# Two transformer-like blocks on one core: the first block's mixers in another order, row-half products as pairs

## The chip, the cores and the metric

The kernel runs on one core of a Trainium2 chip. The metric is the device time of one execution in microseconds (us); the time before is 1532.46 us, the median of three runs (1527.14 to 1532.51). The profile is of one further execution.

## The reference

`reference()` runs `first_block` and then `second_block` on 256 tokens of width 1024, all in float32. `first_block` has two layers, each like this (cut):

```
proj = h @ w_in[l]
nq, nkv, ngate, gq, gk, gv, glr, gog, pu = split(proj)
mixed = concatenate([nsa_mixer(nq, nkv, ngate, ...),
                     gla_mixer(gq, gk, gv, glr, gog, ...),
                     pool_mixer(pu, ...)])
h  = layer_norm(ALPHA * h + mixed @ w_out[l])
ff = square(relu(h @ w_up[l])) @ w_down[l]
h  = layer_norm(ALPHA * h + ff)
```

- `nsa_mixer` (sparse attention; 6 query heads in 2 groups of 3, head size 64) adds three gated attentions per query: over 15 compressed key blocks (a small two-layer network on 32 tokens each), over selected key blocks, and over a window. With 256 tokens all selected blocks and the whole window are kept, so the second and third are plain causal attention, each with its own keys and values.
- `gla_mixer` (linear attention; 6 heads, key size 32, value size 64, chunks of 64 tokens) computes per chunk masked scores times values, adds the decayed queries times the state carried from the chunks before, normalizes, and multiplies by `silu(og)`.
- `pool_mixer` is a windowed mean and a small product.

`second_block` works on 272 tokens: a layer of gated recurrence with windowed attention (16 heads), a mamba2 layer, and a convolutional feed-forward in each.

## The kernel before

**Dense products.** Every product with a large weight is done in three matmuls on split numbers (`mm3`, L273 to L275: high by high, low by high, high by low). A weight piece is loaded by SyncE's one DMA queue into `raw` (3 buffers), ScalarE rounds it to its high part `wh` (L258) and VectorE subtracts to get the low part `wl` (L259), 6 buffers each. `weights()` fixes the order of the pieces, and each `wchunk` call in the code must take the next one. Each `mm3` on 128x128x256 takes one k-slice of a product; 8 of them make a column group of the input projection.

**The mixers' stage of a layer** computes the input projection in groups: `tok(n)` gives a token-major result (1: query, 0: keys, 2: values of the sparse attention, 3: values `gv` of the linear attention), `fm(n)` a feature-major one (8: gate input, 0: values to be compressed, 4 to 6: the output gate `og`). `hooks` are functions called between the k-steps of a group; `behind` wraps them in `issue_after(self.pe.ins)`, which makes everything issued in them stand after the last dense product in the order. Around the change the code reads:

```
tok(2, ..., {HOOKS[3]: blocks, HOOKS[4]: hidden, HOOKS[6]: lambda: self.gla_ends(gq, G)})
tok(3, ..., {HOOKS[5]: compressed})
self.gla_back(l, G, gv, gos)
self.nsa(l, qT, kT, vsb, vc, sg, mh, ml)
for p in range(3): fm(4 + p, ...)        # then gate, times gos, split into mh, ml
self.gemm(a[f"wouta{l}"], 5, 2, mh[:, 0:5], ...)
self.gemm(a[f"woutb{l}"], 3, 4, mh[:, 5:8], ...)
```

So `gla_back` and `nsa` are written in one piece each, and the scheduler, which orders each engine's instructions by their readiness, fills the gaps with dense products of `fm(4..6)` and of `wouta` as it can. `wouta` needs the pooled and linear parts of `mixed`, `woutb` the sparse attention.

**The thin products**, those that use a part of TensorE's rows or columns. `gla_back`: chunk sums (L874, 64x64), scores (L892, 32 rows: `ge` by `gx`), values and states (L902, L908), sums of squares (L916). `nsa`, for each half t of the queries and each head h: scores of the two groups g=0 and g=1 (L796, 64 rows each, at rows 0 to 63 and 64 to 127, into the PSUM banks `a` and `d`), exponentials on VectorE (L801, L805, L806, L811) and ScalarE (L803), transposes (L755), copies of the transposed (L816), and the outputs (L820, 64 columns per group). The second block's attention does its scores in the same two row halves (L1420).

Of the kernel before, what the change touches and what calls it, by code (L numbers as in the profile page):

```python
# [143 lines left out]
def weights(a):  # L144
# [35 lines left out]
class Kern:  # L180
# [267 lines left out]
    def mix1(self, l, h, xh, xl, finish):  # L448
# [57 lines left out]
        def fm(n, evac):  # L506
            (wh, wl), = self.wchunk(a[f"winf{l}"][n])
            ps = self.mbank()[:, :256]
            for k in range(8):
                s = slice(k * 128, k * 128 + 128)  # L510
                self.mm3(ps, wh[:, s], wl[:, s], xh[:, k], xl[:, k], k == 0, k == 7)
            evac(ps)
# [100 lines left out]
        ksb = p1.tile([128, 2, 6, 64], F32, name="ksb", tag="gos")  # L613
        tok(0, lambda t, ps: A.activation(ksb[:, t].rearrange("p a b -> p (a b)"), ps[:, :384], AF.Copy),
            {HOOKS[0]: front, HOOKS[1]: lambda: to_T(qT, qsb), HOOKS[2]: pooled})
        rope(ksb)
        kT = p1.tile([128, 3, 256], F32, name="kT", tag="kT")
        vcT = p1.tile([128, 256], F32, name="vcT", tag="vcT")
        fm(0, lambda ps: A.activation(vcT, ps, AF.Copy))

# [42 lines left out]

        vsb = p1.tile([128, 2, 256], F32, name="vsb", tag="vsb")
        tok(2, lambda t, ps: A.activation(vsb[:, t], ps[:, :256], AF.Copy), {HOOKS[3]: blocks, HOOKS[4]: hidden, HOOKS[6]: lambda: self.gla_ends(gq, G)})
        gv = p1.tile([128, 2, 384], F32, name="gv", tag="tb")
        tok(3, lambda t, ps: A.activation(gv[:, t], ps[:, :384], AF.Copy), {HOOKS[5]: compressed})
# [4 lines left out]
        big = p1.tile([128, 2048], F32, name="big", tag="cw1")  # L672
        gs = big[:, 0:768].rearrange("p (a t) -> p a t", a=3)
        for p in range(3):
            og = w1.tile([128, 256], F32, name="og", tag="og")
            fm(4 + p, lambda ps, og=og: A.activation(og, ps, AF.Copy))
# [3 lines left out]
            V.tensor_tensor(gs[:, p], gs[:, p], gos[:, p], op=OP.mult)  # L680
            self.split(mh[:, 2 + p], ml[:, 2 + p], gs[:, p])
# [6 lines left out]
        self.gemm(a[f"wouta{l}"], 5, 2, mh[:, 0:5], ml[:, 0:5], first, shift)  # L688
# [3 lines left out]
    def gemm(self, chunks, nk, per, xh, xl, sink, shift=None, N=256, bank=None):  # L692
# [59 lines left out]
    def nsa(self, l, qT, kT, vsb, vc, sg, mh, ml):  # L752
# [5 lines left out]
        for t in range(2):  # L758
            W = 128 * (t + 1)
            q = slice(t * 128, t * 128 + 128)  # L760

            P = w1.tile([128, 6, 16], F32, name="pc", tag="pc")
            sc = self.bank()
            for h in range(3):
                mm(sc[:, h * 32:h * 32 + 32], lhsT=qT[:, h, q], rhs=self.kcb, start=True, stop=True)
# [12 lines left out]
            o = self.bank("c")  # L778
            ct = self.bank()
            tr(ct[0:96, 0:128], P.rearrange("p s n -> p (s n)"))  # L780
# [3 lines left out]
            mm(o[:, 0:384], lhsT=vc, rhs=self.cTb.rearrange("p h q -> p (h q)"), start=True, stop=False,  # L784
               skip_group_check=True)
            nb = 2 * (t + 1)
            for h in range(3):

                sp = [self.bank(x) for x in ("a", "d")]
                P = (w1.tile([128, 512], F32, name="P", tag="P", bufs=3),  # L790
                     p1.tile([128, 512], F32, name="Pg", tag=f"tb{h % 2}"))
                m = w1.tile([128, 2, 2], F32, name="m2", tag="m2", bufs=4)
                sm = w1.tile([128, 2, 2], F32, name="s2", tag="s2", bufs=4)
                for b in range(2):
                    for g in range(2):
                        mm(sp[g][:, b * W:b * W + W], lhsT=qT[gp[g], h, q], rhs=kT[gp[g], 1 + b, 0:W], start=True, stop=True)  # L796
                for b in range(2):
                    for g in range(2):
                        c = slice(b * W, b * W + W)

                        V.tensor_tensor_reduce(P[g][:, c], sp[g][:, c], nm[:, 128 * t:128 * t + W], scale=-0.125,  # L801
                                               scalar=3.0e38, op0=OP.add, op1=OP.min, accum_out=m[:, b, g:g + 1])
                        A.activation(P[g][:, c], P[g][:, c], AF.Exp, scale=-1.0, bias=m[:, b, g:g + 1],  # L803
                                     accum_out=sm[:, b, g:g + 1])
                V.reciprocal(sm, sm)  # L805
                V.tensor_tensor(sm, sm, view(sg, t * 18 + 6 + 2 * h, [[6, 2], [1, 2]]), op=OP.mult)  # L806
                PT = []
                for g in range(2):
                    for b in range(2):
                        c = slice(b * W, b * W + W)  # L810
                        V.tensor_scalar(P[g][:, c], P[g][:, c], sm[:, b, g:g + 1], None, op0=OP.mult)  # L811
                    pt = self.bank("b")
# [3 lines left out]
                    A.activation(PT[g][:, :2 * W], pt[:, :2 * W], AF.Copy)  # L816
                for j in range(nb):
                    b, kb = j // (t + 1), j % (t + 1)
                    for g in range(2):
                        mm(o[gp[g], h * 128:h * 128 + 128], lhsT=vsb[:, kb, b * 128 + g * 64:b * 128 + g * 64 + 64],  # L820
                           rhs=PT[g][:, j * 128:j * 128 + 128], start=False, stop=j == nb - 1, skip_group_check=True)
            ov = o[:, 0:384].rearrange("p (h q) -> p h q", h=3)
            self.split(mh[:, 5:8, q], ml[:, 5:8, q], ov)
# [41 lines left out]
    def gla_back(self, l, G, gv, gos):  # L865
# [4 lines left out]
        for n in range(3):  # L870
            b = self.bank()
            r = slice((n % 2) * 64, (n % 2) * 64 + 64)
            for p in range(3):
                mm(b[0:64, p * 128:p * 128 + 128], lhsT=kt[r, n // 2, p * 64:p * 64 + 64],  # L874
                   rhs=gv[r, n // 2, p * 128:p * 128 + 128], start=True, stop=True)
            for i in range(2):
                d = slice(i * 32, i * 32 + 32)
                o = S[d, n, :, i * 64:i * 64 + 64]
                ds = b[d, 0:384].rearrange("p (a v) -> p a v", a=3)[:, :, i * 64:i * 64 + 64]
# [910 lines left out]
```

## Time and profile before

| what | before |
|---|---|
| median of three runs | 1532.46 us (1527.14 to 1532.51) |
| the profiled execution | 1528.76 us |
| its span in the trace | 1526.8 us (2.0 us lie outside) |
| TensorE busy | 1498.2 us, 98% of the span |
| VectorE, ScalarE busy | 1121.6 us (73%), 989.3 us (65%) |
| mixers' stage, layer 1 | 35.43 to 144.12 us: 108.69 us at a mean granted clock of 0.92 |
| mixers' stage, layer 2 | 365.99 to 478.71 us: 112.72 us at 0.88 |

Busy time of TensorE says that a matmul was under way, not that the array worked at its full rate: the granted clock (1.00 is 2.4 GHz, 0.50 is 1.2 GHz) and the shape of the products decide how much was done in it. The two stages go from the first 384-wide product of `tok(1)` to the first product of `woutb`.

### The profile page before, as it was taken

How to read it: one execution, taken by the hardware profiler on the slowest of the kernel's cores; microseconds unless marked ns; L12 is line 12 of the kernel's file. 1: busy time of each engine (PE TensorE's matmuls, PEld its weight loads, DVE VectorE, ACT ScalarE, POOL GpSimd, SP SyncE). 2: the span in 40 equal slices, each digit the busy share in tenths (PEclk: the TensorE clock that was granted, in tenths of full speed). 3: DMA queues.
4: the chain of work that ended last, by engine and by line, in shares of the span. 5: the costliest groups of instructions: out<-in, count | busy, mean ns of one | idle time of the engine just before them, and what ended most of it. 6: DMA issues, size and time to landing. Idle time of an engine off the chain costs nothing.

```text
span 1526.8 us, 29217 instructions
## 1 busy us (share of the span) xinstructions
PE 1498.2 (98%) x11685; PEld 1420.7 (93%) x11685; DVE 1121.6 (73%) x2237; ACT 989.3 (65%) x1922; POOL 3.2 (0%) x11
## 2 busy tenths in 40 slices
PE   8999999999999999999999999999999999999998
PEld 8878999999879999999977999999989999999998
DVE  5847976559657965568774799854898896899853
ACT  5646854448456754457866598754799795598752
POOL 0000000000000000000000000000000000000000
PEclk9979999999889999999989999999999999999999
DMA  7503465545313555445331345544455544345551
GB/s 257 192 21 132 150 219 184 193 159 170 97 42 137 199 190 190 173 162 198 118 111 56 138 164 195 167 175 146 145 190 210 171 138 158 139 148 194 205 176 52
DMA packets 43559, 239.05 MB, mean 157 GB/s; under 512 B 6272, under 2 KB 11296, under 8 KB 20384
## 3 DMA queue, kind: packets, MB, share of 16 engines
q1 hardware_dynamic: 42912, 235.39, 44.6%
q8 instruction: 91, 1.49, 0.4%
q10 hardware_dynamic: 512, 1.80, 0.4%
q14 instruction: 44, 0.36, 0.1%
HBM read 236.09 MB, written 1.08 MB: 155 GB/s over the span
## 4 chain that ended last, share of the span: by engine, by line
PE 87%; DVE 5%; ACT 5%; DMA 1%; issue 1%; SPq 0%; DVEq 0%; ACTq 0%
PE mm L273 10%; PE mm L274 10%; PE mm L275 10%; PE a L273 6%; PE a L274 6%; PE a L275 6%; PE c L274 3%; PE c L275 3%; PE c L273 3%; PE b L275 3%; PE b L274 3%; PE b L273 3%; DVE wl L259 1%; PE d L273 1%; PE d L275 1%; PE d L274 1%
## 5 line engine op out<-in xcount | busy, mean ns | idle before, releaser
L259 DVE TENSOR_TENSOR wl<-raw,wh 128x1024 fp32r<-128x1024 f32 (+3 forms) x448 | 518.3, 1163 | 224.5 <-ACT wh L258 216.6
L258 ACT ACTIVATE wh<-raw 128x1024 fp32r<-128x1024 f32 (+3 forms) x448 | 449.8, 1009 | 313.9 <-PE mm L274 130.3
L275 PE MATMUL mm<-xh,wl 128*128 128x256 f32 (+2 forms) x584 | 171.6, 294 | 1.4 <-DVE wl L259 1.4
L273 PE MATMUL mm<-xh,wh 128*128 128x256 f32 (+2 forms) x584 | 170.9, 293 | 2.1 <-ACT wh L258 2.1
L274 PE MATMUL mm<-xl,wh 128*128 128x256 f32 (+2 forms) x584 | 170.6, 292 | 0.0
L275 PEld LDWEIGHTS mm<-xh,wl 128*128 128x128 f32 x584 | 113.2, 194 | 5.3 <-issue 2.4
L273 PEld LDWEIGHTS mm<-xh,wh 128*128 128x128 f32 x584 | 113.0, 194 | 5.3 <-ACT wh L258 3.3
L274 PEld LDWEIGHTS mm<-xl,wh 128*128 128x128 f32 x584 | 112.6, 193 | 3.6 <-issue 2.8
L273 PE MATMUL a<-xh,wh 128*128 128x256 f32 (+2 forms) x376 | 106.5, 285 | 1.7 <-ACT xh L1101 1.5
L274 PE MATMUL a<-xl,wh 128*128 128x256 f32 (+2 forms) x376 | 107.2, 286 | 0.0
L275 PE MATMUL a<-xh,wl 128*128 128x256 f32 (+2 forms) x376 | 106.4, 284 | 0.0
L275 PE MATMUL mm<-hh,wl 128*128 128x256 f32 (+1 forms) x292 | 82.7, 283 | 0.0
L274 PE MATMUL mm<-hl,wh 128*128 128x256 f32 (+1 forms) x292 | 82.6, 283 | 0.0
L273 PE MATMUL mm<-hh,wh 128*128 128x256 f32 (+1 forms) x292 | 82.6, 283 | 0.0
L275 PE MATMUL a<-hh,wl 128*128 128x256 f32 (+1 forms) x280 | 79.3, 283 | 0.0
L273 PE MATMUL a<-hh,wh 128*128 128x256 f32 (+1 forms) x280 | 79.1, 282 | 0.0
L274 PE MATMUL a<-hl,wh 128*128 128x256 f32 (+1 forms) x280 | 79.0, 282 | 0.0
L273 PEld LDWEIGHTS a<-xh,wh 128*128 128x128 f32 x376 | 70.7, 189 | 2.9 <-ACT xh L1101 2.6
L274 PEld LDWEIGHTS a<-xl,wh 128*128 128x128 f32 x376 | 70.8, 188 | 0.5 <-DVE xl L1102 0.2
L275 PEld LDWEIGHTS a<-xh,wl 128*128 128x128 f32 x376 | 70.9, 189 | 0.1
L273 PE MATMUL mm<-sz,wh 128*128 128x258 f32 (+1 forms) x208 | 62.0, 298 | 0.4 <-ACT yn L1130 0.3
L275 PE MATMUL mm<-sz,wl 128*128 128x258 f32 (+1 forms) x208 | 59.2, 285 | 0.6 <-DVE wl L259 0.6
(634 smaller groups left out, 4625.9 us busy)
## 6 DMA issues: line engine op xcount, KB each, us to landing
raw<-fupb SPq DMA_DIRECT2D x40, 1024.0 KB, 4.8
raw<-wdn SPq DMA_DIRECT2D x32, 1024.0 KB, 4.8
raw<-wupb SPq DMA_DIRECT2D x28, 1024.0 KB, 4.8
raw<-bin SPq DMA_DIRECT2D x22, 1024.0 KB, 4.9
raw<-fdna SPq DMA_DIRECT2D x16, 1024.0 KB, 4.8
raw<-ain SPq DMA_DIRECT2D x11, 1024.0 KB, 4.8
raw<-win SPq DMA_DIRECT2D x8, 768.0 KB, 4.9
raw<-fdnb SPq DMA_DIRECT2D x8, 768.0 KB, 4.3
```

The costliest lines, as they stand in the source:

```text
L258: nc.scalar.activation(h, raw[:, s:s + piece], AF.Copy)
L259: nc.vector.tensor_tensor(l, raw[:, s:s + piece], h, op=OP.subtract)
L273: mm(out, lhsT=lh, rhs=rh, start=first, stop=False, **kw)
L274: mm(out, lhsT=lh, rhs=rl, start=False, stop=False, **kw)
L275: self.pe = mm(out, lhsT=ll, rhs=rh, start=False, stop=last, **kw)
```

## The change

Three things change in the first block, for both layers, and one in both blocks.

1. The weight groups stand in another order: `tok(3)` comes before `tok(0)`, `fm(4..6)` before `tok(2)`.
2. `gla_back` returns seven functions (states, then scores, outputs and norms of each half) that are called as hooks inside `fm(0)`, `fm(4..6)` and `tok(2)`; `nsa` becomes a generator whose steps (compressed scores, scores of a head, transposes, outputs) are called inside `tok(2)` and, after the k-steps 1 and 4 of each of the 8 outputs, inside `wouta`'s product (`between`). The scores run two heads ahead of the transposes.
3. In the first half the transposes of both groups go to one bank, and one copy takes them.
4. `pair(f)` emits `f(1)` and makes `f(0)` stand after it. It is used for the scores and outputs of `nsa` and for the second block's scores. The banks of the scores are named per head ("dd", "cb", "da", "ad").

```
@@ weights
         yield f"winf{l}", 8, 1024
+        yield from tok(3)
         yield from tok(0)
-        yield f"winf{l}", 0, 1024
+        for n in (0, 4, 5, 6):
+            yield f"winf{l}", n, 1024
         yield from tok(2)
-        yield from tok(3)
-        for n in (4, 5, 6):
-            yield f"winf{l}", n, 1024
...
+    def pair(self, f):
+        with self.tc.issue_after(f(1).ins):
+            f(0)
...
@@ mixers
-        tok(0, ..., {HOOKS[0]: front, HOOKS[1]: lambda: to_T(qT, qsb), HOOKS[2]: pooled})
...
-        tok(2, ..., {HOOKS[3]: blocks, HOOKS[4]: hidden, HOOKS[6]: lambda: self.gla_ends(gq, G)})
-        tok(3, ..., {HOOKS[5]: compressed})
-        self.gla_back(l, G, gv, gos)
-        self.nsa(l, qT, kT, vsb, vc, sg, mh, ml)
...
+        tok(3, ..., {0: front, 5: lambda: to_T(qT, qsb)})
+        tok(0, ..., {2: pooled, 6: lambda: self.gla_ends(gq, G)})
+        rope(ksb)
+        gla = self.gla_back(l, G, gv, gos)
+        run = lambda *n: lambda: [gla[i]() for i in n]
+        fm(0, lambda ps: A.activation(vcT, ps, AF.Copy), {4: run(0)})
...
+        fm(4, lambda ps: gate(0, ps), {0: run(1), 4: blocks})
+        fm(5, lambda ps: gate(1, ps), {0: run(2), 3: hidden, 6: run(4)})
+        fm(6, lambda ps: gate(2, ps), {0: run(3), 2: run(5), 5: compressed})
+        nsa = self.nsa(l, qT, kT, vsb, vc, sg, mh, ml)
+        step = lambda: next(nsa, None)
+        tok(2, ..., {0: last_gla, 2: step, 4: step, 6: step})
...
-        self.gemm(a[f"wouta{l}"], 5, 2, mh[:, 0:5], ml[:, 0:5], first, shift)
+        self.gemm(a[f"wouta{l}"], 5, 2, mh[:, 0:5], ml[:, 0:5], first, shift, between=lambda: behind(step))
+        for _ in nsa:
+            pass
...
@@ gemm
+                        if between and k in (1, 4):
+                            between()
...
@@ nsa: scores of a head
-                sp = [self.bank(x) for x in ("a", "d")]
+            sp = [self.bank(x) for x in ("dd", "cb", "da", "ad", "ad", "ad")[3 * t + h]]
...
-                for b in range(2):
-                    for g in range(2):
-                        mm(sp[g][:, b * W:b * W + W], lhsT=qT[gp[g], h, q], rhs=kT[gp[g], 1 + b, 0:W], ...)
+            for b in range(2):
+                self.pair(lambda g: mm(sp[g][:, b * W:b * W + W], lhsT=qT[gp[g], h, qs[t]],
+                                       rhs=kT[gp[g], 1 + b, 0:W], ...))
...
@@ gla_back
-            be = [self.bank() for _ in range(2)]
+            be = [self.bank("da"[1 - t]) for _ in range(2)]
...
+        return [states, on(scores, 0), on(outputs, 0), on(norms, 0), on(scores, 1), on(outputs, 1), on(norms, 1)]
```

Three places of TensorE's queue, in layer 1, show what moves; a row is line, operation, out<-in, shape, with the engines that it waits for in brackets and the number of equal rows behind. The first is where the linear attention's scores stand. Before (L892: scores of the first half, `d` their bank; L874 chunk sums; L796 sparse-attention scores; L274 and so on dense):

```order
L796 MATMUL a_946<-kT_573,qT_275 128x128
L874 MATMUL d_854<-gv_761,gkt_457 64x128 [waits DVE_49,PE_49,Activation_49]
L874 MATMUL d_854<-gv_761,gkt_457 64x128 x2
L796 MATMUL a_946<-kT_573,qT_275 128x128
L796 MATMUL a_984<-kT_573,qT_275 128x128
L892 MATMUL d_862<-ge_456,gx_454 128x128 [waits DVE_49,PE_49]
L892 MATMUL d_862<-ge_456,gx_454 128x128 x2
L796 MATMUL a_984<-kT_573,qT_275 128x128
L274 MATMUL mm_1233<-xl_75,wh_798 128x256
L275 MATMUL mm_1233<-xh_74,wl_799 128x256
L273 MATMUL mm_1233<-xh_74,wh_798 128x256
L892 MATMUL d_863<-ge_456,gx_454 128x128 [waits DVE_49,PE_49]
```

After, the scores are L967 and the dense products L272 to L274:

```order
L272 MATMUL mm_723<-xh_74,wh_662 128x256
L273 MATMUL mm_723<-xl_75,wh_662 128x256
L274 MATMUL mm_723<-xh_74,wl_663 128x256 [waits DVE_49]
L967 MATMUL a_727<-ge_459,gx_457 128x128 [waits Activation_49]
L967 MATMUL a_728<-ge_459,gx_457 128x128 [waits Activation_49]
L967 MATMUL a_727<-ge_459,gx_457 128x128
L967 MATMUL a_728<-ge_459,gx_457 128x128
L967 MATMUL a_727<-ge_459,gx_457 128x128
L967 MATMUL a_728<-ge_459,gx_457 128x128
L272 MATMUL mm_723<-xh_74,wh_662 128x256
L273 MATMUL mm_723<-xl_75,wh_662 128x256
```

The products of the two banks (727 and 728) alternate, and dense products stand ahead of them and behind them; before, the three of one bank stood together among other thin products.

The second place is the sparse attention's scores of the second half of the queries. Before, the left half of the heads (bank `a`) and, 130 rows later, the right half (bank `d`):

```order
L796 MATMUL a_1085<-kT_573,qT_275 128x256 [waits DVE_49]
L796 MATMUL a_1085<-kT_573,qT_275 128x256
L796 MATMUL a_1131<-kT_573,qT_275 128x256 [waits DVE_49]
L796 MATMUL a_1131<-kT_573,qT_275 128x256
```

```order
L755 MATMUL d_1079<-ident_87,pc_1062 96x128 [waits DVE_49]
L796 MATMUL d_1086<-kT_573,qT_275 128x256 x2
L796 MATMUL d_1132<-kT_573,qT_275 128x256 [waits PE_49,Activation_49]
L784 MATMUL c_1078<-cTb_132,vc_614 128x384 [waits DVE_49]
L796 MATMUL d_1132<-kT_573,qT_275 128x256
L796 MATMUL d_1178<-kT_573,qT_275 128x256 [waits DVE_49]
L796 MATMUL d_1178<-kT_573,qT_275 128x256
```

After (L825 scores, L867 outputs, L777 transposes), one head's scores:

```order
L825 MATMUL d_1237<-kT_429,qT_275 128x256 [waits DVE_49]
L867 MATMUL c_1174<-PT_1221,vsb_436 64x128 [waits Activation_49]
L867 MATMUL c_1174<-PT_1221,vsb_436 64x128 x3
L825 MATMUL a_1236<-kT_429,qT_275 128x256
L825 MATMUL d_1237<-kT_429,qT_275 128x256
L825 MATMUL a_1236<-kT_429,qT_275 128x256
L777 MATMUL b_1260<-ident_87,pc_1112 96x128 [waits DVE_49,PE_49]
```

The two halves of a head, 1236 and 1237, now stand in one place; in this head another head's outputs stand behind the first of the four.

The third place is one head inside `wouta`'s product. Before (L755 transposes, L820 outputs):

```order
L755 MATMUL b<-ident,P 128x128 [waits DVE_49]
L755 MATMUL b<-ident,P 128x128
L755 MATMUL b<-ident,P 128x128 [waits DVE_49]
L755 MATMUL b<-ident,P 128x128
L755 MATMUL b<-ident,Pg 128x128 [waits DVE_49,Activation_49]
L755 MATMUL b<-ident,Pg 128x128
L755 MATMUL b<-ident,Pg 128x128 [waits DVE_49]
L755 MATMUL b<-ident,Pg 128x128
L820 MATMUL c<-PT,vsb 64x128
L273 MATMUL mm<-mh,wh 128x256 [waits Activation_49]
L273 MATMUL mm<-mh,wh 128x256
L820 MATMUL c<-PT,vsb 64x128 [waits Activation_49]
L820 MATMUL c<-PT,vsb 64x128 x6
```

After:

```order
L777 MATMUL b<-ident,P 128x128 [waits PE_49,Activation_49]
L777 MATMUL b<-ident,P 128x128 [waits DVE_49]
L777 MATMUL b<-ident,Pg 128x128 [waits DVE_49] x2
L272 MATMUL mm<-mh,wh 128x256
L273 MATMUL mm<-ml,wh 128x256
L274 MATMUL mm<-mh,wl 128x256
L272 MATMUL mm<-mh,wh 128x256
L273 MATMUL mm<-ml,wh 128x256
L274 MATMUL mm<-mh,wl 128x256
L272 MATMUL mm<-mh,wh 128x256
L273 MATMUL mm<-ml,wh 128x256
L274 MATMUL mm<-mh,wl 128x256
L825 MATMUL d<-kT,qT 128x256
L825 MATMUL a<-kT,qT 128x256
```

Before, the transposes of both groups and the outputs follow each other with two dense products among them; now nine dense products and the first scores of another head stand between the transposes and the outputs.

## Rows read from the trace of the kernel before

**Rows 1.** The page's head.

```profile
span 1526.8 us, 29217 instructions
```

**Rows 2.** Busy time by stretch: us, each engine's busy time, granted clock, DMA share, GB/s.

```profile
35.43:46.56 11.13, 11.13 (x64) 9.68 (x61) 9.84 (x20) 7.46 (x16) 0.00 (x0) 1.00 0.86 306
70.22:76.41 6.19, 5.93 (x44) 4.55 (x43) 5.10 (x16) 1.77 (x6) 0.00 (x0) 1.00 0.57 200
76.41:93.48 17.07, 17.07 (x66) 12.35 (x65) 4.30 (x14) 3.75 (x14) 0.00 (x0) 0.50 0.00 0
97.75:134.50 36.75, 35.39 (x249) 26.73 (x248) 25.45 (x112) 26.59 (x81) 0.00 (x0) 1.00 0.22 73
134.50:144.12 9.62, 9.62 (x82) 9.52 (x81) 7.16 (x11) 3.89 (x6) 0.00 (x0) 1.00 0.40 126
407.51:434.81 27.30, 27.30 (x110) 22.18 (x110) 6.96 (x24) 7.16 (x20) 0.00 (x0) 0.50 0.04 9
35.43:144.12 108.69, 106.19 (x734) 88.06 (x732) 72.77 (x210) 61.34 (x155) 0.00 (x0) 0.92 0.34 113
365.99:478.71 112.72, 110.67 (x734) 92.26 (x732) 72.18 (x208) 61.72 (x156) 0.00 (x0) 0.88 0.28 92
```

**Rows 3.** TensorE's timeline, layer 1, 73.7 to 74.6 us: start, us, line, out<-in, count.

```profile
73.73 0.90 PE L892 MATMUL d<-ge,gx 32*128 32x128 f32 x6
74.57 0.48 PE L796 MATMUL a<-kT,qT 64*128 64x128 f32 x2
```

**Rows 4.** TensorE's timeline, layer 1, 104 to 124 us.

```profile
104.32 1.16 PE L796 MATMUL d<-kT,qT 64*128 64x128 f32 x8
105.40 0.39 PE L275 MATMUL mm<-xh,wl 128*128 128x256 f32 x1
...
114.89 0.28 PE L275 MATMUL mm<-mh,wl 128*128 128x256 f32 x1
...
116.79 1.81 PE L796 MATMUL d<-kT,qT 64*128 64x256 f32 x6
118.53 0.91 PE L784 MATMUL c<-cTb,vc 96*128 96x384 f32 x2
119.37 1.56 PE L796 MATMUL d<-kT,qT 64*128 64x256 f32 x6
120.86 0.39 PE L273 MATMUL mm<-mh,wh 128*128 128x256 f32 x1
121.08 0.28 PE L274 MATMUL mm<-ml,wh 128*128 128x256 f32 x1
121.20 0.28 PE L275 MATMUL mm<-mh,wl 128*128 128x256 f32 x1
...
121.74 0.70 PE L755 MATMUL b<-ident,P 128*128 128x128 f32 x4
...
124.51 1.09 PE L820 MATMUL c<-PT,vsb 128*64 128x128 f32 x14
```

**Rows 5.** TensorE's timeline, second block's attention.

```profile
768.73 0.39 PE L1420 MATMUL a<-akT,aqT 64*128 64x272 f32 x1
768.74 0.39 PE L1420 MATMUL d<-akT,aqT 64*128 64x272 f32 x1
768.96 0.39 PE L1420 MATMUL a<-akT,aqT 64*128 64x272 f32 x1
```

**Rows 6.** ScalarE's timeline, layer 1, one head of the second half.

```profile
119.44 0.49 ACT L803 ACTIVATE Pg<-Pg,m 128x256 f32<-128x256 f32 x1
...
122.47 0.60 ACT L816 ACTIVATE PT<-b 128x512 f32<-128x512 f32 x1 [0.80 <-PE b L755]
```

**Rows 7.** VectorE's timeline, the same stretch.

```profile
118.31 0.42 DVE L801 CUSTOM_DVE_ANT_0 Pg<-d,nmask 128x256 f32<-128x256 f32 x1
...
120.45 0.17 DVE L805 RECIPROCAL s<-s 128x4 f32<-128x4 f32 x1
...
121.33 0.61 DVE L811 TENSOR_SCALAR P<-P,s 128x256 f32<-128x256 f32 x2
```

More of the change, by code (lines that the diff above doesn't have):

```diff
@@ L511, in fm @@
                 self.mm3(ps, wh[:, s], wl[:, s], xh[:, k], xl[:, k], k == 0, k == 7)
+                if k in hooks:
+                    behind(hooks[k])
             evac(ps)
@@ L679, in mix1, with gated, last_gla @@
             V.scalar_tensor_tensor(gs[:, p], og, self.v(f"ng{l}", p), gs[:, p], op0=OP.mult, op1=OP.mult)
-            V.tensor_tensor(gs[:, p], gs[:, p], gos[:, p], op=OP.mult)
-            self.split(mh[:, 2 + p], ml[:, 2 + p], gs[:, p])
+        def gated():
+            for p in range(3):
+                V.tensor_tensor(gs[:, p], gs[:, p], gos[:, p], op=OP.mult)
+                self.split(mh[:, 2 + p], ml[:, 2 + p], gs[:, p])
+        fm(4, lambda ps: gate(0, ps), {0: run(1), 4: blocks})
[3 more added lines that the diff above has]
+        step = lambda: next(nsa, None)
+        def last_gla():
+            gla[6]()
+            gated()
+        tok(2, lambda t, ps: A.activation(vsb[:, t], ps[:, :256], AF.Copy), {0: last_gla, 2: step, 4: step, 6: step})
         first, shift, add, stats, finish = self.layernorm(self.nrm, h, f"ln1_g{l}", f"ln1_b{l}", xh, xl, nd=6)
@@ L757, in nsa, with compressed @@
         gp = [slice(g * 64, g * 64 + 64) for g in range(2)]
-        for t in range(2):
-            W = 128 * (t + 1)
-            q = slice(t * 128, t * 128 + 128)
+        qs = [slice(t * 128, t * 128 + 128) for t in range(2)]
+        state, o = {}, {}
+        def compressed(t):
             P = w1.tile([128, 6, 16], F32, name="pc", tag="pc")
-            sc = self.bank()
+            sc = self.bank("b")
             for h in range(3):
-                mm(sc[:, h * 32:h * 32 + 32], lhsT=qT[:, h, q], rhs=self.kcb, start=True, stop=True)
+                mm(sc[:, h * 32:h * 32 + 32], lhsT=qT[:, h, qs[t]], rhs=self.kcb, start=True, stop=True)
             V.scalar_tensor_tensor(P, sc[:, 0:96].rearrange("p (s n) -> p s n", n=16), 0.125,
@@ L783, in nsa, with begin @@
                 A.activation(self.cTb[r, h], ct[r, 0:128], AF.Copy)
[L784 removed]
+        def begin(t):
+            o[t] = self.bank("c")
+            mm(o[t][:, 0:384], lhsT=vc, rhs=self.cTb.rearrange("p h q -> p (h q)"), start=True, stop=False,
                skip_group_check=True)
[L786 to L812 removed]
@@ new lines, in transposes @@
+        def transposes(t, h):
+            W, nb = 128 * (t + 1), 2 * (t + 1)
+            P, PT = state[t, h], []
+            if t == 0:
+                pt = self.bank("b")
+                for g in range(2):
+                    for j in range(2):
+                        tr(pt[:, g * 256 + j * 128:g * 256 + j * 128 + 128], P[g][:, j * 128:j * 128 + 128])
+                T = p1.tile([128, 512], F32, name="PT", tag=("gq", "gk")[h % 2])
+                A.activation(T, pt, AF.Copy)
+                PT = [T[:, 0:256], T[:, 256:512]]
+            else:
+                for g in range(2):
+                    pt = self.bank("bd"[g])
@@ L815, in nsa, with outputs, end @@
                     PT.append(p1.tile([128, 512], F32, name="PT", tag=("gq", "gk")[g]))
[L816 to L823, printed above, removed]
+                    A.activation(PT[g], pt, AF.Copy)
+            state[t, h] = PT
+        def outputs(t, h):
+            nb, PT = 2 * (t + 1), state[t, h]
+            for j in range(nb):
+                b, kb = j // (t + 1), j % (t + 1)
+                self.pair(lambda g: mm(o[t][gp[g], h * 128:h * 128 + 128],
+                                       lhsT=vsb[:, kb, b * 128 + g * 64:b * 128 + g * 64 + 64],
+                                       rhs=PT[g][:, j * 128:j * 128 + 128], start=False, stop=j == nb - 1,
+                                       skip_group_check=True))
+        def end(t):
+            self.split(mh[:, 5:8, qs[t]], ml[:, 5:8, qs[t]], o[t][:, 0:384].rearrange("p (h q) -> p h q", h=3))
+        compressed(0)
+        scores(0, 0)
+        yield
+        scores(0, 1)
+        yield
+        compressed_T(0)
+        compressed(1)
+        yield
+        heads = [(t, h) for t in range(2) for h in range(3)]
+        for i, (t, h) in enumerate(heads):
+            transposes(t, h)
+            yield
+            if h == 0:
+                begin(t)
+            outputs(t, h)
+            if h == 2:
+                end(t)
+            if i + 2 < 6:
+                scores(*heads[i + 2])
+            if i == 1:
+                compressed_T(1)
+            yield
     def gla_front(self, l, gq, gk, glT, wg2, rst):
@@ L1418, in attend @@
                 for i in range(per):
-                    for kv in range(2):
-                        mm(sc[kv][:, i * W:i * W + W], lhsT=qT[KP[kv], hb * 4 + i0 + i, q0:q0 + 128],
-                           rhs=kT[KP[kv], keys[kv]], start=True, stop=True)
+                    self.pair(lambda kv: mm(sc[kv][:, i * W:i * W + W], lhsT=qT[KP[kv], hb * 4 + i0 + i, q0:q0 + 128],
+                                            rhs=kT[KP[kv], keys[kv]], start=True, stop=True))
                 for i in range(per):
```

96 lines of the change are left out of this document (61 added, 35 removed).

## The prediction

> **What bounds the kernel now.** I read the page's head first: the span is 1526.8 us [rows 1], the execution 1528.76 us, so about 2 us lie outside. TensorE is busy for 98% of the span, so a gain must come from TensorE work that becomes shorter, not from idle time that is filled. The busy time by stretch says where it can: the mixers' stage takes 108.69 us in layer 1 and 112.72 us in layer 2, at mean granted clocks of 0.92 and 0.88 [rows 2]. That mean hides two levels. In 76.41 to 93.48 us the clock is 0.50 (1.2 GHz) for 17.07 us, in layer 2 in 407.51 to 434.81 us for 27.30 us; the stretch after is at 1.00 (2.4 GHz) again. In both, TensorE counts as busy for all of the time, while VectorE is busy for 4.30 and 6.96 us, ScalarE for 3.75 and 7.16 us: nothing waits for them for long. In the 6.19 us ahead of the first fall TensorE was busy for 5.93 us at 1.00, but with thin products (the linear attention's 64x64 and 32-row ones, the left halves of the sparse scores) and few dense ones among them [rows 2].
>
> The second loss is in TensorE's timeline. The sparse scores use 64 of 128 rows. The eight 64x128 rows at 104.32 us go on until 105.40, 0.135 us each; the six 64x256 rows at 116.79 until 118.53 and those at 119.37 until 120.86, 0.29 and 0.25 us each [rows 4]: each half pays for the whole array. In the second block the same form, 64 rows by 272, starts in both banks within 0.01 us (768.73 `a`, 768.74 `d`) and the next at 768.96: 0.23 us for two rows [rows 5].
>
> **The change part by part.**
>
> *Weight groups and linear attention as steps.* Nothing is added to TensorE: the dense products are the same, the thin ones too. They are spread: the 64x64 sums, scores, values and norms go into `fm(0)`, `fm(4..6)` and `tok(2)`, with dense products between them. If the clock stays at 1.00, both stretches run in half of their time: (17.07 + 27.30)/2 = 22.2 us gained [rows 2]. Bounds: 0 (it falls elsewhere) and 22.2. I take all of it, because the place that made it fall, a long series of thin products with hardly a dense one, is gone; the nearest series that is left is as short as the one from 115.0 (behind the dense product at 114.89) to 120.86 us, 5.9 us with transposes, outputs and half-row scores and no dense product [rows 4], and the stretch in which it lies kept 1.00 [rows 2].
>
> *Order of the loads.* `tok(3)` moves ahead of `tok(0)`, so that three groups of 384 columns follow each other, about 6 MB together with their neighbours on SyncE's queue. In 35.43 to 46.56 us, where such groups run now, TensorE is busy for 11.13 of 11.13 us with DMA at 0.86 and 306 GB/s [rows 2]: 6 MB take 19.6 us at that rate, about as long as their products. I take 0; without that cover it would cost some 1.5 us.
>
> *Score pairs.* Per layer there are 24 rows of 128 columns at 0.135 us (3.2 us) and 24 of 256 at 0.27 (6.5 us) [rows 4]. A perfect pair costs one row in place of two. In the new order a few heads are split (another head's outputs or transposes stand among the four products), so that the 12 products of a half (three heads, two branches, two groups) take the time of 7 instead of 6. So 5/12 of 9.7 us, 4.05 per layer, 8.1 in all. Bounds: 0 (the halves run one after the other) and 9.7.
>
> *Linear scores alternate.* The six 32-row products at 73.73 us take 0.84 us until 74.57, 0.14 each [rows 3]; 24 per layer are 3.4 us. Now two row groups in two banks alternate. No row shows a 32-row pair, so the bounds are 0 and half of both layers' 6.8, 3.4 us; I take the middle, 1.7, as the 64-row pair of rows 5 is the nearest row and the first pair of each group may start late.
>
> *Output pairs.* The fourteen rows at 124.51 us take 1.09 us, 0.08 each [rows 4]: less than the 0.135 of a score of the same 128 columns, so the column halves overlap already. 0.
>
> *Mode switches.* A dense product behind a thin group starts its successor 0.22 us later (120.86 to 121.08), where dense ones behind each other take 0.12 (to 121.20) [rows 4]: 0.1 us per switch. In the two queues a layer's stage has 31 changes from thin to dense now and 34 before: 0.3 us per layer, which I leave out.
>
> *New waits.* TensorE takes its queue in order, and each head's chain now lies between its scores and its transposes. For a head of the second half it is: a reduce on VectorE of 0.42 us, then four exponentials of 0.49 (the other reduces lie beside them), a reciprocal of 0.17 and a product of that size, and two pairs of scales at 0.61 [rows 6, 7]; 3.9 us, and behind the transposes 0.60 for each copy [rows 6]. What stands on TensorE between a head's scores and its transposes is another head's transposes, four for each group (2 x 0.7) and outputs (1.1), and about fifteen dense products, one output's worth (1.8 at 0.117, from 82 in 9.62 us) [rows 2, 4]: 4.3 us. So cover and chain are nearly equal. ScalarE and VectorE also make the next `wh` and `wl` there. Queued behind a waiting transpose are the dense products of the same output, and behind them everything. Bounds: 0 and 15 us per layer (six heads by 2.5 us, a chain whose half is not covered). I take 2 per layer, 4 in all, as the rows put cover and chain within 0.4 us of each other, a third of a microsecond for each of six heads.
>
> *Copies and second block.* One copy instead of two for three heads per layer saves some 0.5 us of ScalarE off the path: 0. In the second block the halves already start together [rows 5]: 0, plus or minus 1.
>
> Sum: 22.2 + 8.1 + 1.7 - 4 = 28.0 us. Against the profiled execution: 1528.76 - 28 = 1500.8, say **1501 us**. The median shown, 1532.46, is 3.7 us above that execution, so 1501 may be measured up to that much higher; the range holds it. From below it fits: the layer-1 stage would be 108.69 - 8.5 - 4.05 - 0.85 + 2, about 97 us, the layer-2 stage 112.72 - 13.65 - 2.9, about 96: two stages of the same work become equal.
>
> **The rivals.**
> 1. *The clock falls at another place* (a series of linear steps behind each other, or the 64x30 products of `hidden`). For: the fall came with TensorE at work for 5.93 of the 6.19 us before it [rows 2]. Against: the 5.9 us of thin work at 1.00 [rows 4]. If half of the clock's gain or all of it is lost, 1512 to 1523 us.
> 2. *Transposes pull the clock down.* In the new order the transposes of five heads stand in `wouta`'s product, some 17 us per layer (8 outputs of 15 products at 0.117 and the thin work). If half of that ran at 0.50, it would cost 8.5 us per layer: 1501 + 17 = 1518. Against: four transposes at 121.74 [rows 4] lie in a stretch at 1.00. The Trainium skill ("TensorE: Matmul & The Clock Gate", Part 4) says that the full clock does not engage for transposes; this is what that would do here, and the rows so far don't bear it out.
> 3. *ScalarE and VectorE set the pace* of the heads: 5 to 12 us per layer instead of 2, 1507 to 1521. For: in 97.75 to 134.50 us they are busy for 26.59 and 25.45 of 36.75 us [rows 2], and the stage gets shorter with the same work on them. Against: neither is full.
> 4. *The pairs don't overlap* because the first waits for its bank: 8.1 + 1.7 lost, 1511. Against: rows 5.
> 5. *Slower: a rigid queue.* With the heads' steps nailed behind named products, each of the 12 heads could expose its whole chain of 5.1 us (3.9 and two copies of 0.60): 61 us, 1501 + 61 = 1562. It decides from 28/12, about 2.3 us exposed per head. Against: two heads run ahead, and the cover of 4.3 us.
> 6. *It doesn't do what it says*: the fall of the clock is not due to the series of thin products and comes whatever the order, and waits eat the pairs: about 1528.
>
> **How the numbers follow.** The forecast (1493 to 1508) has 0.58, rival 1 0.11, rival 2 0.03, rival 3 0.13, rival 4 0.04, rival 5 0.05, rival 6 0.01; 0.05 are for better than 1493 (no waits at all, full pairs: 1528.76 - 22.2 - 9.7 - 3.4 = 1493.5, and TensorE's idle time in the stages, 2.5 and 2.05 us, filled: 1489). The range 1487 to 1520 leaves out rivals 5 and 6 and the upper ends of 1 and 3, and little below. 0.5% of the time, 7.7 us, is about what a measurement of this kernel can tell from no change: faster by more than that 0.90, within it 0.05 (rival 6, the top of rivals 1 and 3), slower 0.05 (rival 5).
>
> **What would show it.** In the profile after, both mixers' stages at a granted clock of 1.00 and of about 96 us each show the first step; scores of `a` and `d` that start within 0.01 us of each other, with 0.135 and 0.27 us for a pair, the second; idle time of TensorE ahead of the transposes and outputs (L777, L867) of at most some 2 us per layer, the waits. A stretch at 0.50 in either stage, or idle times of over 1 us ahead of each head's transposes with VectorE or ScalarE as what ended them, would prove it wrong, and so would a gain that lies outside of the two stages.

## The result and the profile after

The changed kernel takes 1487.61 us (median of four runs, 1484.61 to 1491.44) against 1529.80 us before (1526.01 to 1532.51): a ratio of 0.9727 (95% interval 0.9691 to 0.9763), 41.8 us less. The forecast was 1501 us, 28 us less. The time lies below the forecast's own 1493 to 1508 us, in the corner that had a chance of 0.05, and 0.6 us inside the lower end of the range; the four runs differ by more than that among each other, so that it lies inside is partly luck.

The busy time by stretch of the changed kernel (us, each engine's busy time, granted clock, DMA share, GB/s), first the two mixers' stages, then the second block's attention:

```profile
33.23:125.81 92.58, 88.40 (x735) 76.44 (x732) 72.08 (x210) 60.51 (x151) 0.00 (x0) 1.00 0.41 140
347.61:439.34 91.73, 88.48 (x735) 76.57 (x733) 71.23 (x208) 60.87 (x153) 0.00 (x0) 1.00 0.34 116
728.98:762.26 33.28, 30.61 (x218) 21.10 (x218) 25.25 (x107) 21.31 (x61) 0.00 (x0) 1.00 0.28 100
```

The stages are at 1.00 from end to end, 92.58 and 91.73 us where [rows 2] have 108.69 at 0.92 and 112.72 at 0.88. The attention stretch of before is this:

```profile
768.39:805.40 37.01, 35.03 (x219) 24.67 (x219) 25.06 (x106) 21.23 (x61) 0.00 (x0) 0.86 0.24 88
```

The difference of the two spans, 1526.8 less 1482.8, is then made up so: ahead of layer 1's stage 2.2 us (of it 1.7 for a stretch of 3.4 us at 0.50, at 21.8 us before and gone after), layer 1's stage 16.1, layer 2's stage 21.0, the second block's attention 3.7, the rest 1.0.

TensorE's timeline of the changed kernel, layer 1: linear scores (L967), sparse scores (L825), outputs (L867), transposes (L777).

```profile
61.63 0.94 PE L967 MATMUL a<-ge,gx 32*128 32x128 f32 x12
...
106.70 0.48 PE L825 MATMUL d<-kT,qT 64*128 64x256 f32 x1
106.71 0.48 PE L825 MATMUL a<-kT,qT 64*128 64x256 f32 x1
107.02 0.38 PE L825 MATMUL d<-kT,qT 64*128 64x256 f32 x1
107.03 0.38 PE L825 MATMUL a<-kT,qT 64*128 64x256 f32 x1
107.33 0.38 PE L316 MATMUL mm<-c,minus 128*128 128x256 f32 x1
...
108.26 0.60 PE L777 MATMUL b<-ident,P 128*128 128x128 f32 x4
108.70 0.60 PE L777 MATMUL d<-ident,Pg 128*128 128x128 f32 x4
109.06 0.37 PE L272 MATMUL mm<-mh,wh 128*128 128x256 f32 x1
...
120.78 1.09 PE L867 MATMUL c<-PT,vsb 128*64 128x128 f32 x16
121.80 0.38 PE L316 MATMUL mm<-c,minus 128*128 128x256 f32 x1
```

Four 64x256 rows in two banks take 0.63 us until L316 begins, against six in 1.74 and 1.49 us one by one [rows 4]; twelve linear scores take 0.87 us until the next row, against six in 0.84 [rows 3]; eight transposes take 0.80 us, and outputs stand in groups of 8 or 16.

For the sizes I took, from all of TensorE's rows of a stage, the time from each row's start to the next one's, with half of the time where the clock was 0.50. What is left is the work at full clock (a wait counts with the row ahead of it):

| us in a stage, at full clock | before, layer 1 | after | before, layer 2 | after |
|---|---|---|---|---|
| sparse scores (48 rows) | 10.47 | 7.25 | 10.49 | 7.25 |
| sparse outputs (72) | 7.21 | 4.84 | 7.21 | 4.83 |
| transposes (38) | 5.91 | 3.82 | 5.89 | 3.83 |
| linear scores (24) | 2.85 | 1.73 | 2.85 | 1.73 |
| other linear products | 7.63 | 6.15 | 7.45 | 6.15 |
| all rows | 100.16 | 92.57 | 99.09 | 91.73 |
| of these, TensorE idle | 2.50 | 4.18 | 2.05 | 3.25 |

So of 37.1 us in the stages 22.2 are the clock (8.5 and 13.7) and 14.9 are shorter work (7.6 and 7.4), although idle time grew. Two more profiles of the same old first block, with other stretches at 0.50, give 99.5 to 100.5 us for all rows of layer 1 and 99.1 and 99.95 for layer 2, so this reckoning holds to about 1 us.

### The profile page after: what moved, and what is told of

Its sections match the earlier page's. It is cut to its first block, busy times and chain, and to the rows that moved or that the text cites. A ratio compares the mean times of both kernels' runs of the same rounds, so it can differ in the third digit from the quotient of the medians.

```text
span 1482.8 us, 29196 instructions
## 1 busy us (share of the span) xinstructions
PE 1453.7 (98%) x11685; PEld 1390.7 (94%) x11685; DVE 1119.8 (76%) x2237; ACT 987.4 (67%) x1916; POOL 3.2 (0%) x11
## 4 chain that ended last, share of the span: by engine, by line
PE 87%; ACT 6%; DVE 5%; DMA 1%; issue 1%; DVEq 0%; SPq 0%; ACTq 0%
PE mm L272 10%; PE mm L274 10%; PE mm L273 10%; PE a L272 7%; PE a L273 7%; PE a L274 7%; PE c L273 3%; PE c L274 3%; PE c L272 3%; PE b L272 3%; PE b L274 3%; PE b L273 3%; DVE wl L258 1%; PE d L272 1%; PE d L274 1%; PE d L273 1%
## 5 line engine op out<-in xcount | busy, mean ns | idle before, releaser
L272 PE MATMUL mm<-xh,wh 128*128 128x256 f32 (+2 forms) x584 | 170.1, 292 | 1.0 <-ACT wh L257 1.0
L274 PE MATMUL mm<-xh,wl 128*128 128x256 f32 (+2 forms) x584 | 168.2, 288 | 2.5 <-DVE wl L258 2.5
L273 PE MATMUL mm<-xl,wh 128*128 128x256 f32 (+2 forms) x584 | 167.2, 286 | 0.0
L274 PEld LDWEIGHTS mm<-xh,wl 128*128 128x128 f32 x584 | 111.2, 190 | 4.8 <-DVE wl L258 3.2
L272 PEld LDWEIGHTS mm<-xh,wh 128*128 128x128 f32 x584 | 110.9, 190 | 4.7 <-ACT wh L257 1.6
L273 PEld LDWEIGHTS mm<-xl,wh 128*128 128x128 f32 x584 | 111.0, 190 | 1.1 <-issue 0.5
L272 PE MATMUL a<-xh,wh 128*128 128x256 f32 (+2 forms) x376 | 107.0, 287 | 1.7 <-ACT xh L1186 1.5
L273 PE MATMUL a<-xl,wh 128*128 128x256 f32 (+2 forms) x376 | 107.6, 287 | 0.0
L274 PE MATMUL a<-xh,wl 128*128 128x256 f32 (+2 forms) x376 | 106.7, 285 | 0.0
L274 PE MATMUL mm<-hh,wl 128*128 128x256 f32 (+1 forms) x292 | 82.7, 283 | 0.0
L273 PE MATMUL mm<-hl,wh 128*128 128x256 f32 (+1 forms) x292 | 82.6, 283 | 0.0
L272 PE MATMUL mm<-hh,wh 128*128 128x256 f32 (+1 forms) x292 | 82.6, 283 | 0.0
L274 PE MATMUL a<-hh,wl 128*128 128x256 f32 (+1 forms) x280 | 79.3, 283 | 0.0
L273 PE MATMUL a<-hl,wh 128*128 128x256 f32 (+1 forms) x280 | 79.1, 282 | 0.0
L272 PE MATMUL a<-hh,wh 128*128 128x256 f32 (+1 forms) x280 | 79.0, 282 | 0.0
L272 PEld LDWEIGHTS a<-xh,wh 128*128 128x128 f32 x376 | 71.3, 190 | 2.9 <-ACT xh L1186 2.6
L273 PEld LDWEIGHTS a<-xl,wh 128*128 128x128 f32 x376 | 71.2, 189 | 0.5 <-DVE xl L1187 0.2
L274 PEld LDWEIGHTS a<-xh,wl 128*128 128x128 f32 x376 | 71.2, 190 | 0.1
L272 PE MATMUL mm<-sz,wh 128*128 128x258 f32 (+1 forms) x208 | 61.9, 298 | 0.5 <-ACT yn L1215 0.3
L274 PE MATMUL mm<-sz,wl 128*128 128x258 f32 (+1 forms) x208 | 59.1, 285 | 0.6 <-DVE wl L258 0.6
```

## The experiments

Theory A: the long series of thin products, with half-row scores as the only other work between the linear attention's steps, pulled the clock down; dense products between them hold it. Theory B: the pairs hold it. Theory C: where it falls is an accident of the execution.

**The kernel before again** (no edit).

> The kernel before once more, for a second profile. Theory A and B: the same low stretches in both first-block stages, 17 and 27 us, give or take a few. Rival C (where the clock falls is an accident of the moment in each execution): stretches at other places, of other lengths; the sum of the time at 0.50 then differs from the 61 us of the first profile by more than 10 us.

1526.78 us. TensorE was at 0.50 in 74.45 to 91.52 (17.07 us), 405.54 to 432.85 (27.31), 770.77 to 781.01 (10.24) and 811.73 to 815.14 us: the same places and lengths as in the first profile but for the 3.4 us at 21.8. C falls for the places of the long stretches; their lengths are less fixed, as the run with pairs in the second block alone shows.

**The linear attention in one piece, pairs kept.**

```
-fm(0, ..., {4: run(0)});  fm(4, ..., {0: run(1), 4: blocks});  ...
+fm(0, ..., {});  fm(4, ..., {4: blocks});  ...
 def last_gla():
-    gla[6]()
+    for f in gla: f()
```

> The changed kernel with the seven steps of the linear attention called in one piece at the place of the last (in the first k-step of tok(2)); order of the weights, the sparse attention's steps and the pairs stay. Theory A: the thin products stand in a series again, so the clock falls to 0.50 in both stages; if for the 17 to 27 us of before, 22 us are lost: 1505 to 1512 us, and VectorE's part of the chain adds waits. Rival B (pairs hold the clock): both stages stay at 1.00 and only waits are added, 1489 to 1497 us.

1520.05 us, ratio 0.9951 (0.9926 to 0.9976). The two long stretches:

```profile
93.00:113.48 20.48, 17.48 (x72) 13.46 (x73) 7.85 (x40) 7.39 (x26) 0.00 (x0) 0.50 0.00 0
427.50:441.16 13.66, 11.02 (x46) 8.89 (x45) 5.73 (x31) 5.93 (x22) 0.00 (x0) 0.50 0.00 0
```

With the pairs in place the clock falls again, as A says. Here TensorE also waited (17.48 of 20.48 us busy, and a wait of 1.17 us ended as the first stretch began), so this run alone doesn't part thin work from idle time; before did, with 17.07 of 17.07 us busy [rows 2].

**Before, without pairs, the sparse attention held behind the linear attention.**

```
-self.gla_back(l, G, gv, gos)
-self.nsa(l, qT, kT, vsb, vc, sg, mh, ml)
+end = self.gla_back(l, G, gv, gos)       # the last matmul of L916
+with self.tc.issue_after(end.ins):
+    self.nsa(l, qT, kT, vsb, vc, sg, mh, ml)
```

> The kernel before, with no pairs, but the whole sparse attention stands behind the last product of the linear attention (one named edge), so that only dense products can fill the linear attention's gaps; the left and right halves of the scores still stand apart. Theory A (what pulled the clock down are the thin products of the linear attention with half-row scores of the left half between them and hardly a dense one): the long stretches of 17 and 27 us are gone, at most a few of 3.4 us are left; the scores keep their single price of 10 us per layer, so a gain of about 20 of the pairs' 32: 1505 to 1512 us. Theory B (it is the pairs as such, two halves at once, that hold the clock): the clock falls for 15 us or more in each stage, 1520 to 1535 us.

1508.53 us, ratio 0.9852 (0.9833 to 0.9870), 22 us less. The stages, and TensorE in the linear attention (L893 its scores, L917 its norms, L903 and L909 its outputs, L273 to L275 dense):

```profile
34.58:137.10 102.52, 100.36 (x734) 84.81 (x732) 74.12 (x211) 63.43 (x159) 0.00 (x0) 0.98 0.38 124
358.89:459.37 100.48, 99.16 (x735) 83.19 (x733) 71.71 (x208) 61.49 (x156) 0.00 (x0) 1.00 0.31 104
```

```profile
81.55 0.88 PE L917 MATMUL d<-gsq,ones 128*128 128x384 f32 x2
82.36 1.67 PE L893 MATMUL d<-ge,gx 32*128 32x128 f32 x12
83.96 0.39 PE L275 MATMUL mm<-xh,wl 128*128 128x256 f32 x1
84.28 0.43 PE L903 MATMUL d<-azero,gv 128*64 128x128 f32 x2
84.64 0.39 PE L273 MATMUL mm<-xh,wh 128*128 128x256 f32 x1
...
85.65 0.87 PE L903 MATMUL d<-azero,gv 128*64 128x128 f32 x10
86.45 1.55 PE L909 MATMUL d<-ge,S 64*128 64x64 f32 x12
87.93 0.38 PE L274 MATMUL mm<-xl,wh 128*128 128x256 f32 x1
```

This is the cleanest test. The linear products are the same single ones (twelve scores in 1.60 us, 82.36 to 83.96), no row is paired by name, the scores still take 9.6 us per layer; what changed is that dense products fill the gaps. The only stretch at 0.50 in a stage was one of 3.4 us at 40.03, far ahead of the linear attention. A holds, B is not needed. Layer for layer the work at full clock is no shorter than before (100.8 and 100.5 us), so the gain in the stages is the clock's. What the run doesn't part: the half-row scores left this stretch as the dense products came in.

**The changed kernel without named pairs.**

```
 def pair(self, f):
-    with self.tc.issue_after(f(1).ins):
-        f(0)
+    f(0)
+    f(1)
```

> The changed kernel, but the two halves of a pair are issued without a named order between them (first block's scores and outputs, second block's scores). Theory A (the series of thin products of the linear attention pulled the clock down, and spreading them holds it; pairs only save their overlap): both mixers' stages stay at a granted clock of 1.00, no stretch at 0.50 in them; the scores lose part of 3.2 us per layer where halves separate again, so 1489 to 1497 us. Rival B (pairs hold the clock, since half-row products one by one leave half of the array idle): stretches at 0.50 come back in the first block's stages or in the second block's attention, 10 to 25 us, so 1500 to 1512 us. For the second block alone: B gives back the 5 us there, A gives nothing.

1491.9 us, ratio 0.9765 (0.9720 to 0.9810); the interval overlaps with the changed kernel's. The linear attention's stretch kept 1.00, and the scores took 7.25 us per layer as with the pairs: where a head is a step of its own, its halves stand together without being told. One stretch is new, in layer 1 beside `tok(3)`:

```profile
36.45:43.28 6.83, 6.83 (x18) 4.59 (x18) 5.59 (x14) 4.48 (x7) 0.00 (x0) 0.50 1.05 370
```

It came at this place, 6.8 us each, in three more profiles of kernels with the new order of the weights and in no profile of before; it is 3.4 us that the forecast did not have, when it falls. A wait stands ahead of it, for the gate input `glT` from ScalarE:

```profile
36.30 1.86 PE L909 MATMUL d<-glT,sml 16*64 16x256 f32 x4 [2.11 <-ACT glT L579]
```

In the four profiles with the 6.8 us this wait took 1.41 to 2.11 us; with the linear attention in one piece it took 1.27, and 3.4 us at 0.50 followed; in the four profiles without a fall here it took 0.93 us in one and at most 0.12 in three. So this stretch goes with idle time of TensorE, other than the long ones of before; no run moved the wait alone.

**Before with the pairs alone** (the edit of `pair` and its three uses, nothing else).

> The kernel before with nothing changed but the pairs (scores and outputs of the first block, scores of the second); weight order, linear and sparse attention in one piece each as before. Theory A: the 22 us of the clock stay lost in the linear attention's stretch, 8 to 15 us come from pairs and outputs: 1512 to 1522 us. Rival B: the clock stays at 1.00 everywhere and the whole gain but a few us is there: 1485 to 1497 us.

1496.09 us, ratio 0.9804 (0.9756 to 0.9851), 30 us less.

```profile
32.06:130.30 98.24, 93.15 (x735) 79.52 (x733) 73.68 (x211) 61.84 (x157) 0.00 (x0) 0.98 0.39 129
352.12:448.51 96.39, 91.80 (x734) 78.33 (x732) 71.95 (x208) 60.84 (x156) 0.00 (x0) 1.00 0.33 108
```

My number for A was wrong, B's is met to a hair, and yet B does not hold: with every pair kept the clock fell (the linear attention in one piece), and without any it held (the sparse attention held behind). What the edge does is this: in before the left halves, in bank `a`, ran early among the linear products, all of which write banks `d`; the first right half, in bank `d`, came at 102.43 us. With the edge a left half waits for its right half; the first sparse score stands at 91.66 us, behind the whole linear attention, and its gaps get dense products, as with the sparse attention held behind. It is A by another hand. Scores take 7.9 us per layer, outputs 4.8, transposes still 5.9. Of the 26.8 us that the two stages became shorter, 20.5 are the clock and 6.3 shorter work.

**Before with pairs in the second block alone.**

> The kernel before with pairs in the second block's scores alone. If the pairs there take the 10.24 us at 0.50 away: 5 us less, 1521 to 1525 us, the first block's stretches as before. If that stretch is an accident of the moment (it was gone too with the same order of those rows and no named pair): nothing or up to 5 us, with the stretch gone or there independently of the pairs, 1522 to 1529 us. The two are told apart by the profile alone: with the pairs and still a stretch of 5 us or more there, the first falls.

1528.63 us, ratio 0.9982 (0.9968 to 0.9996): 2.8 us less (0.6 to 4.9). The stretch in the attention was 3.4 us long, not 10.24. The first block is untouched here, and TensorE's rows up to the end of layer 2's stage are the same in the same order as in before; yet the long stretches changed their lengths, from 17.07 and 27.30 us to these:

```profile
73.26:103.98 30.72, 30.72 (x121) 24.59 (x122) 8.52 (x30) 8.02 (x24) 0.00 (x0) 0.50 0.04 11
411.18:428.25 17.07, 17.07 (x67) 12.59 (x66) 3.80 (x14) 3.34 (x11) 0.00 (x0) 0.50 0.00 0
```

So the order says that the clock falls in the linear attention, not for how long: 44.4 us together in two executions, 47.8 in this one.

**The changed kernel with the second block's scores unpaired.**

> The changed kernel without the pairs in the second block's scores. If the pairs there remove the stretch of 10.24 us at 0.50 (seen in three of three profiles with the unpaired queue in the old order and in none of the profiles with pairs): it is back, attention there takes 37 instead of 33.3 us, 1489 to 1496 us. Rival (the queue with all pairs undone had none): no stretch longer than 3.4 us, 1484 to 1491 us.

1490.62 us, ratio 0.9748 (0.9718 to 0.9777); one stretch of 3.4 us there, attention 34.1 us. Over all profiles: the old kernel's first block and no pair here 10.24 us (three profiles: before twice, and the one with the sparse attention held behind), no named pair in the changed kernel 0 and 3.4, pairs 0 or 3.4 (nine profiles). In this run the attention's rows stand in the very order of before, where 10.24 us were lost in three profiles; so neither the pairs nor the order of these rows alone decides it, and why the stretch is short here is open.

**The changed kernel with the sparse attention in one piece.**

```
-tok(2, ..., {0: last_gla, 2: step, 4: step, 6: step})
+tok(2, ..., {0: last_gla})
+for _ in nsa: pass
-self.gemm(a[f"wouta{l}"], ..., between=lambda: behind(step))
+self.gemm(a[f"wouta{l}"], ...)
```

> The changed kernel with the sparse attention issued in one piece behind tok(2), not in steps between the products of wouta; linear attention in steps, weight order and pairs stay. Theory A: the clock stays at 1.00 in the linear attention's stretch; a series of 33 thin products of the sparse attention comes up, which may pull it down there; without that, the sparse steps between dense products are worth only their waits and switches: 1487 to 1494 us; with a fall 1494 to 1505 us. Rival: the gain over the kernel before lies in the steps of the sparse attention: 1505 us or more at a clock of 1.00.

1492.96 us, ratio 0.9749 (0.9728 to 0.9770). The clock held in the linear attention and in the series of thin products of the sparse attention. At full clock the stages took 93.5 and 92.9 us against 92.6 and 91.7, so the sparse steps are worth about 2 us; 3.4 us more went to the stretch beside `tok(3)`, which fell in this profile.

**The transposes of both groups in one bank.** `self.bank("bd"[g])` became `self.bank("b")`.

> The changed kernel with both groups' transposes of the second half in one bank, as before. The forecast took the transposes at nothing, and they became 2.1 us per layer shorter. If the second bank did that: transposes and the waits ahead of them go back from 3.8 to 5 to 6 us per layer, 2 to 4 us in all. Rival: the one copy for a first-half head and the steps did it, and the transposes stay at 3.8 to 4.3 us per layer.

1488.09 us, ratio 0.9735 (0.9714 to 0.9757); transposes 4.0 us per layer, against 3.82, although they stood in eleven pieces instead of eight. Neither the second bank nor the number of pieces is what shortened them.

**The remaining waits moved**, first attempt: the two pairs of a head in one chain (the second ordered behind the first), `tok(0)` in banks `mm`, and

```
-fm(5, ..., {0: run(2), 3: hidden, 6: run(4)});  fm(6, ..., {0: run(3), 2: run(5), 5: compressed})
+fm(5, ..., {0: run(2), 4: run(4), 7: hidden});  fm(6, ..., {1: run(3), 3: run(5)})
-tok(2, ..., {0: last_gla, 2: step, 4: step, 6: step})
+tok(2, ..., {0: compressed, 1: last_gla, 3: step, 5: step, 7: step})
```

> The changed kernel with its remaining waits moved: the two pairs of a head in one piece, the banks of tok(0) other than those of tok(3), the hidden layer of the compression four k-steps later, the second half's linear scores two earlier, compressed later. Of the 4.2 and 3.9 us of idle time of TensorE in the two stages I expect half to go, 3 to 4 us: 1482 to 1487 us. Rival: the waits move elsewhere, because ScalarE and VectorE set them: no change within 2 us, 1486 to 1490 us.

1493.49 us, ratio 0.9748 (0.9726 to 0.9769). At full clock layer 2 got 2.0 us shorter, but the clock fell beside the hidden layer's thin products (L641):

```profile
387.55:397.79 10.24, 10.24 (x97) 8.92 (x95) 4.07 (x13) 3.71 (x11) 0.00 (x0) 0.50 0.05 20
```

```profile
386.11 0.93 PE L969 MATMUL d<-ge,gx 32*128 32x128 f32 x10 [1.25 <-ACT gos L992]
...
388.74 3.63 PE L641 MATMUL d<-tb,cw 128*64 128x30 f32 x64
```

The fall at 387.55 us came ahead of the hidden layer and behind a new wait of 1.25 us, so the hidden layer did not begin it. The same wait in layer 1 (1.28 us) brought no fall.

**Second attempt**: the hidden layer's products in two groups with dense ones between, in `fm(5)` at k=3 and 5, `run(3)`, `run(5)` and `compressed` one k-step later in `fm(6)`, and the chain.

> The changed kernel with the two pairs of a head in one piece, the 32 products of the compression's hidden layer in two groups of 16 with dense products between and two k-steps later, the first half's norms and the second half's outputs one k-step later. If what was lost in the earlier attempt is the clock (the hidden layer beside the linear attention's steps), the clock stays at 1.00 in both stages, the scores take 6.6 us per layer instead of 7.25 and 1 to 2 us of waits go: 1482 to 1487 us. Rival: the waits move on and the clock falls for a few us somewhere: 1487 to 1494 us.

1487.13 us, ratio 0.9731 (0.9709 to 0.9752): both stages at 1.00 and no gain over the changed kernel. The wait of 1.25 us was gone too, so this run doesn't show which of the two had cost the clock. The scores stayed at 7.24 us, in the same ten pieces: the chain did not keep other thin work out. No version here beats the changed kernel by more than the measurement tells.

**The changed kernel again** (no edit).

> The changed kernel once more, for a second profile. If the clock's hold is a property of the order: no stretch at 0.50 longer than 3.4 us in the mixers' stages and the second block's attention, 1484 to 1492 us. If it is an accident of the execution: stretches of 7 us or more in one of these places.

1489.0 us, ratio 0.9732 (0.9707 to 0.9758). Stages 94.16 and 91.75 us; four stretches of 3.4 us at 0.50 over the span (22.05, 49.36, 766.16, 1069.94), where the first profile had one (1065.52; the last 2.7 to 5.2 us of every profile are at 0.50 too), and a span of 1487.1 instead of 1482.8 us. No long one came back; the short ones move from execution to execution.

## Why the prediction came out as it did

- **Clock in the stages, 22.2 us: right**, 22.2 measured, and for the reason given: holding dense products between the linear steps is enough without a pair, and a series of them falls again with pairs. Of the size some is luck: another execution of the same first block lost 47.8 us to the two stretches instead of 44.4. None of the six rivals came, with one correction to rival 1: the stretch at 36 to 44 us.
- **Score pairs, 8.1 us: right in kind, too high**, 3.2 per layer, 6.5 in all. A pair of 128 columns takes 0.16 us and one of 256 takes 0.31, not the 0.135 and 0.27 of a single row. Not through `pair` as the forecast had it: in the changed kernel the steps alone set the halves together; in the old one the edge alone does.
- **Linear scores, 1.7 us: right**, 1.1 per layer.
- **New waits, 4 us: near in size by luck, wrong in place.** Idle time grew by 1.7 and 1.2 us, but not in the heads' chains, where the forecast looked for it: ahead of transposes and outputs it fell, in layer 1 from 1.36 to 1.02 us and in layer 2 from 1.17 to 1.01. What grew stands in the projection and the linear attention (us in total, times, longest; after, layer 1, and in the last row before):

```profile
PE a L497 <- ACT gv L669: 0.8, 1, 0.8
PE d L455 <- ACT qT L538: 0.8, 1, 0.8
PE d L998 <- DVE azero L969: 0.6, 1, 0.6
...
PE b L755 <- ACT PT L816: 1.0, 2, 0.7
```

- **Output pairs, 0: the step that failed**, 2.4 us per layer. The price per row inside a long group (0.08 busy) was read, and not that in before the outputs of five of the six heads came in two pieces, as here:

```profile
123.71 0.43 PE L820 MATMUL c<-PT,vsb 128*64 128x128 f32 x2
124.07 0.50 PE L273 MATMUL mm<-mh,wh 128*128 128x256 f32 x2
...
125.53 0.66 PE L755 MATMUL b<-ident,P 128*128 128x128 f32 x4
```

 The two rows of the first piece take 0.36 us until the dense one begins, and the fourteen left take 1.02 (124.51 to 125.53), as long as the whole group of 16 of after (120.78 to 121.80): so a head in two pieces costs 0.36 us more. Five heads of a layer were split so, at 0.35 or 0.36 each, and the sixth lost 0.60 with a wait of 0.17 inside: 2.4 us. Without named pairs two heads were split again, and outputs took 5.55 us instead of 4.84; in the old kernel the edge alone made six pieces of the eleven, at 4.8 us. So the pairs did this, the term that the forecast put at nothing.
- **Copies and transposes, 0: failed too**, 2.1 us per layer, but not for the number of pieces: eleven cost 0.16 us more than eight. About half of it, 1.0 and 0.8 us, is idle time ahead of transposes that went (1.19 and 1.00 us before, 0.18 after). The rest fits another change: in before six transposes stood directly ahead of outputs, 0.20 us until the next start, where one ahead of a dense product takes 0.03; after, none does. No run changes that alone.
- **Mode switches, left out: too coarse.** Changes from thin to dense were counted. Changes between kinds of thin products, as from transposes to outputs, were not.
- **Second block, 0 plus or minus 1: failed**, 3.7 us. The forecast took pairs that already start together as nothing to gain and did not look at the 10.24 us at 0.50 in that place. The gain is 3.7 us and not 5.1, as TensorE's idle time there grew from 1.98 to 2.67 us; the other 0.7 was not parted.
- **Order of the loads, 0: too low**: 1.6 us more in `tok` in layer 1, 0.7 less in layer 2, and the stretch beside `tok(3)` when it falls.

Forecast was 22.2 + 8.1 + 1.7 - 4 = 28.0. Measured in the stages: clock 22.2, scores 6.5, linear scores 2.2, outputs 4.8, transposes 4.1, other linear products 2.8, less 5.5 for dense products, `tok` and the rest with the waits behind them: 37.1. The attention adds 3.7, the rest of the program 3.2, of which 1.1 are fewer short stretches at 0.50. So 6.9 of 44.0 us lie outside of the two stages, which the forecast had named as a sign of being wrong.

## What to carry to other kernels

Look at what fills the gaps of a chain of thin products: if it is more thin work, a busy TensorE can still run at half clock, and one ordering edge that lets dense products in can be worth as much as a rewrite. Two changes that remove the same cause don't add: pairs alone gave 30 us, steps without named pairs 36, both 42 (the last two lie within each other's intervals). Look at the rows at both ends of a thin group, where halves stand alone, and not only at the price per row inside it. Say where a wait will stand and check that place: a term can be right in size and wrong in place.

## What was not expected of the hardware

The clock went to 0.50 with TensorE counted busy in every moment of the stretch (17.07 of 17.07 us), at the same places in two executions; with the same rows in a third, the stretches were 30.72 and 17.07 us long instead of 17.07 and 27.30. Short stretches of 3.4 us at 0.50 stand elsewhere in each execution of the same kernel, one in one profile and four in another. Three stretches more cost half of their 10.2 us, 5.1, enough for the 4.3 us between those two spans.
